# A hybrid encoder layer: the end of the first sweep, with one gate's products ahead of the last chunk's inner products and two pieces of element work behind `Ah`

## The chip, the cores and the metric

The kernel runs on one core of a Trainium2 chip. The core has five engines that each work through a list of instructions of their own, in order: TensorE (PE, with its weight loads shown apart as PEld), VectorE (DVE), ScalarE (ACT), GpSimd (POOL) and SyncE (SP), which here only issues DMAs. The metric is the device time of one execution in microseconds. Before the change it is 1314.11 us, the median of 3 runs from 1314.02 to 1314.79 us.

## The reference, cut to what matters

One layer projects `x` (2048 x 1024) into two groups of heads, mixes tokens in both, and joins them in one output projection and a LayerNorm.

```python
h = x @ w_in
(g_q, g_k, g_v, g_gate, g_lr_f, g_lr_b, m_cq, m_ckv, m_kr, m_gate) = split(h)
o_a = gla_branch(...)          # gated linear attention, forward and backward scans
o_b = mla_branch(...)          # latent attention with softmax
x = layer_norm(ALPHA * x + concat([o_a, o_b]) @ w_out)

# inside the linear attention, per chunk, b = cumsum(log_a):
q_dec, k_dec, k_tail = qc * exp(b), kc * exp(-b), kc * exp(b_last - b)
attn = where(mask, q_dec @ k_dec.T, 0.0)         # the inner products
o_intra = attn @ vc
state = state * exp(b_last) + k_tail.T @ vc
o = rms_norm(o_fwd + o_bwd) * silu(g_gate)
```

## The kernel before, in words

Every float32 product is made of three matmuls on a high and a low part of both operands (`mm3`, lines 420 to 422). ACT writes the high part (`hi`, line 366), and DVE or POOL the difference (`lo`, line 372). A pair therefore costs one ACT instruction and one DVE or POOL instruction, and the names end in `h` and `l`.

The work has three stages. **Sweep A** goes over 16 chunks of 128 positions from the last to the first (`c` from 15 to 0, step `i` from 0 to 15) and makes the projections of the linear attention (`ipa`), its decays, the inner products `Ap`, their masked form `At` with its parts `Ah` and `Al`, the products with the values (`Op`, then `oi`), the chunk's state `Up` and `Us`, and the gate: products `ipg` with the gate weights `wgh`, `wgl`, then the three ACT passes and one DVE pass of SiLU (tile `gs`). Results go to scratch in DRAM. Three gates are left for the end of the sweep: that of chunk 0 (`ipg` on `xah`, `xal`), which runs while the last chunk's own chain is finished, and those of chunks 15 and 14 (`late_gates`, on `xbh`, `xbl`, SiLU tile `ub`). **Sweep C** takes pairs of chunks forward: projections `ipm` and `pz`, the weights `pabs`, and per chunk the state products `Ob` that finish the linear attention. **Attention** and the output projection follow.

Three things set the order of the work around the change. In sweep A the order of writing mostly sets it, and `after(...)` holds what is written inside it behind a named instruction. In `late_gates` the splits of the weights `wm` and `wz`, of the first two input tiles (`xch`, `xcl`), and the SiLU of the two late gates are merged by two written lists, `TAIL_ACT` and `TAIL_DVE`. Sweep C starts behind these lists, ordered by the table `PLACE_C`.

At the end of sweep A, `run("intra", i)` (`ga_intra`, line 979) issues the twelve `Ap` matmuls, `At` on ACT (L987) and on DVE (L989), `Ah` on ACT and `Al` on DVE. Two buffers hold split inputs for the gates, so the split of chunk 14 (`xbh` on ACT, `xbl` on DVE, both 128x1024) goes into the buffer that chunk 0's gate still reads, and waits for that gate's last matmul. `load_x` keeps two raw input tiles, so the load of the second `xcf` waits on SP for `xbl`. POOL's multiplication of `Us` (L1030) follows DVE's `Us` (L1028).

Later names: `wml` and `wzl` are DVE's eight low parts of `wm` and of `wz`; `Sf` and `SU` on POOL (L1387, L1390, L1395) are sweep C's running state and the stored states that come back from DRAM; `MMb` and `qlb` are the operands of `Ob` (L1418, L1419).

Of the kernel before, what the change touches and what calls it, by code (L numbers as in the profile page):

```python
# [22 lines left out]
NCH = S // P  # L23
# [332 lines left out]
class K:  # L356
# [254 lines left out]
    def sweep_a(self):  # L611
        tc, nc, ins, cp = self.tc, self.nc, self.ins, self.cp
        with ExitStack() as ctx:
# [55 lines left out]
            g1 = ctx.enter_context(tc.tile_pool(name="g1", bufs=1))  # L669
# [3 lines left out]
            ch = self.ch = [dict(cst, c=NCH - 1 - i, i=i, lr=lrs[i % 2]) for i in range(NCH)]  # L673
            self.wa = wa
            run = lambda n, i: [0 for _ in getattr(self, "ga_" + n)(ch[i])]
# [24 lines left out]
            for t in ORDER_A.split():  # L700
                n, i = t.split(".")
# [21 lines left out]
            i = NCH - 1  # L723
# [3 lines left out]
            for k in self.gate_products(0, *ch[i]["x"], ip):  # L727
                if k == 5:
                    run("kt", i)
                    run("intra", i)  # L730
            self.gate_end(0, g1)
            run("state", i)
            run("av", i)

# [244 lines left out]
    def ga_intra(self, d):  # L979

        nc, c = self.nc, d["c"]
        Ap = d["gp"].tile([P, H, 2, P], F32, tag="gp", name=f"Ap{c}")
        for h in range(H):
            self.mm3(Ap[:, h], d["kh"][:, h], d["kl"][:, h], d["qbh"][:, h], d["qbl"][:, h])
        yield
        At = self.t512(d, "At")
        nc.scalar.activation(At, Ap[:, :, 1], AF.Copy)  # L987
        yield
        nc.vector.copy_predicated(At, d["mask"][:, None, :].to_broadcast([P, H, P]), Ap[:, :, 0])  # L989
        yield  # L990
        Ah = d["Ah"] = self.t512(d, "Ah", dt=F32R)
        self.hi(Ah, At)
        yield
        Al = d["Al"] = self.t512(d, "Al", dt=F32R)
        self.lo(Al, At, Ah)
        yield
# [62 lines left out]
    def late_gates(self):  # L1059

        tc, nc, ins, bc = self.tc, self.nc, self.ins, self.bc
        self.xch = bc.tile([P, NK, 2, P], F32R, name="xch")
        self.xcl = bc.tile([P, NK, 2, P], F32R, name="xcl")
        self.wqr_h = bc.tile([P, 2, 256], F32R, name="wqr_h")
        self.wqr_l = bc.tile([P, 2, 256], F32R, name="wqr_l")
        self.wabs_h = bc.tile([P, 2, H, P], F32R, name="wabs_h")
        self.wabs_l = bc.tile([P, 2, H, P], F32R, name="wabs_l")
        wm = self.load_ws(self.wm, [ins["wB"][k, :, 512:960] for k in range(NK)], 448, "wm")
        wz = self.load_ws(self.wz, [ins["wB"][k, :, 960:1472] for k in range(NK)], 512, "wz")
        next(wm)  # L1070
        with self.part("x14"):
            self.xlate.append(self.split_x(self.xab, self.xraw, NCH - 2, "xb", "dve"))
        next(wz)
        xc = self.load_x(0, "xc", 2)
        with self.part("wm"):
            self.Wm = next(wm)
        self.late_gate(NCH - 1, *self.xlate[0], self.ip)
        with self.part("c0"):
            self.split_c(xc[0], 0, "dve")
        with self.part("c1"):  # L1080
            self.split_c(xc[1], 1, "dve")
        self.late_gate(NCH - 2, *self.xlate[1], self.gp)
        with self.part("wz"):
            self.Wz = next(wz)
        self.tail = {e: self.merge(e, names) for e, names in zip(ENGINES[1:], (TAIL_ACT, TAIL_DVE))}
# [923 lines left out]
```

## Time and profile before

| | |
|---|---|
| median of the runs | 1314.11 us (1314.02 to 1314.79) |
| the profiled execution | 1313.98 us |
| its span | 1312.0 us |
| PE busy | 1288.9 us, 98% |
| DVE busy | 963.2 us, 73% |
| ACT busy | 812.9 us, 62% |
| POOL busy | 785.0 us, 60% |
| granted TensorE clock | 0.998 |
| sweep A's last steps and late gates | about 355 to 373 us of the span |

The busy shares are means over stages with different limits. In a row of the timeline the first number is the start in us from the span's begin, the second the duration in us; then come the engine, the line, the operation, the tiles written and read, the shapes, and in brackets the idle time before it with what ended that wait. Neighbouring rows of one kind are merged into one, with their count behind an x. Matmuls overlap one another, so their spacing is read from their starts.

### The profile page before, as it was taken

What the parts mean: (1) busy time and instruction counts of PE and PEld (TensorE: products, weight loads), DVE (VectorE), ACT (ScalarE), POOL (GpSimd) and SP (SyncE); (2) the same over time, 40 slices, a digit from 0 to 9 for tenths busy, and PEclk for the clock granted to TensorE, in tenths of its full rate; (3) what the DMA queues carried; (4) which work ended last, traced back from release to release, by engine and by line L of the source; (5) the groups of instructions that cost most, each with busy time, mean ns of one, the idle gap of its engine ahead of it and who ended that gap; (6) DMA issues with size and microseconds to landing.
All of it is one profiled execution on the core that took longest, in us unless ns stands there. A gap on an engine that the chain in (4) does not pass through costs nothing.

```text
span 1312.0 us, 19984 instructions
## 1 busy us (share of the span) xinstructions
PE 1288.9 (98%) x7081; PEld 1130.2 (86%) x7081; DVE 963.2 (73%) x1712; ACT 812.9 (62%) x1339; POOL 785.0 (60%) x494
## 2 busy tenths in 40 slices
PE   7999999999999999999999999999999999999997
PEld 7999999999889999999788888888888887788886
DVE  7967685655675455555888888888888888469997
ACT  6765656555575656664787877888888888511110
POOL 0143333232467666671388888889999999764441
PEclk9999999999999999999999999999999999999999
DMA  8132313132475555655401111122223110576662
GB/s 283 63 99 55 92 53 93 49 80 66 152 245 173 193 192 177 204 198 184 114 1 41 41 42 41 41 57 64 58 70 101 48 41 9 89 234 200 216 193 97
DMA packets 107819, 145.81 MB, mean 111 GB/s; under 512 B 17250, under 2 KB 62694, under 8 KB 107720
## 3 DMA queue, kind: packets, MB, share of 16 engines
q1 hardware_dynamic: 99128, 142.41, 35.3%
q0 software_dynamic: 672, 2.10, 0.4%
q8 instruction: 56, 0.92, 0.3%
q10 hardware_dynamic: 7920, 0.03, 0.3%
q14 instruction: 43, 0.35, 0.2%
HBM read 94.14 MB, written 50.36 MB: 110 GB/s over the span
## 4 chain that ended last, share of the span: by engine, by line
PE 65%; ACT 2%; POOL 1%; DMA 1%; DVE 1%; issue 0%; SPq 0%; DVEq 0%; ACTq 0%; POOLq 0%
PE pS L1521 4%; PE pS L1524 4%; PE pS L1523 4%; PE pS L1525 4%; PE o L420 4%; PE pS L1522 4%; PE o L422 4%; PE o L421 4%; PE po L421 2%; PE po L422 2%; PE po L420 2%; PE pz L421 2%; PE pz L420 2%; PE pz L422 2%; PE ipm L422 2%; PE ipm L420 2%
## 5 line engine op out<-in xcount | busy, mean ns | idle before, releaser
L372 POOL TENSOR_TENSOR pl<-s,ph 128x1024 fp32r<-128x1024 f32 x128 | 306.8, 2411 | 67.0 <-ACT ph L366 61.8
L1543 DVE TENSOR_TENSOR rm<-pS,rm 128x512 f32<-128x512 f32 x210 | 144.9, 690 | 44.2 <-ACT s L1530 39.0
L1530 ACT ACTIVATE s<-pS 128x1024 f32<-128x1024 f32 x128 | 131.4, 1026 | 67.9 <-PE pS L1525 65.9
L1567 DVE TENSOR_TENSOR s<-s,mb 128x1024 f32<-128x1024 f32 x128 | 151.2, 1213 | 9.5 <-PE mb L1561 9.3
L1030 POOL TENSOR_TENSOR Us<-Us,cw 128x512 f32<-128x512 f32 x16 | 18.5, 1157 | 226.7 <-DVE Us L1028 174.9
L366 ACT ACTIVATE ph<-s 128x1024 fp32r<-128x1024 f32 x128 | 135.0, 1056 | 16.7 <-PE o L422 16.1
L1571 ACT ACTIVATE s<-s 128x1024 f32<-128x1024 f32 x128 | 131.4, 1050 | 13.8 <-DVE s L1567 13.7
L420 PE MATMUL ipa<-wah,xah 128*128 128x384 f32 (+1 forms) x384 | 130.9, 341 | 6.1 <-ACT wah L366 5.9
L422 PE MATMUL ipa<-wah,xal 128*128 128x384 f32 (+1 forms) x384 | 125.3, 326 | 0.0
L421 PE MATMUL ipa<-wal,xah 128*128 128x384 f32 (+1 forms) x384 | 124.9, 325 | 0.0
L1521 PE MATMUL pS<-qh,ckvT_h 128*128 128x512 f32 x256 | 103.7, 405 | 0.7 <-ACT s L1571 0.4
L420 PE MATMUL o<-ph,vh 128*128 128x512 f32 x256 | 102.6, 401 | 0.0
L422 PE MATMUL o<-ph,vl 128*128 128x512 f32 x256 | 101.3, 396 | 0.0
L1524 PE MATMUL pS<-rh,krs 128*128 128x512 f32 x256 | 101.2, 395 | 0.0
L421 PE MATMUL o<-pl,vh 128*128 128x512 f32 x256 | 101.1, 395 | 0.0
L1523 PE MATMUL pS<-qh,ckvT_l 128*128 128x512 f32 x256 | 100.9, 394 | 0.0
L1525 PE MATMUL pS<-rl,krs 128*128 128x512 f32 x256 | 100.7, 393 | 0.0
L1522 PE MATMUL pS<-ql,ckvT_h 128*128 128x512 f32 x256 | 100.6, 393 | 0.0
L1594 DVE TENSOR_TENSOR ap<-ap,s 128x512 f32<-128x512 f32 x120 | 83.1, 692 | 7.0 <-ACT s L1571 5.1
L372 POOL TENSOR_TENSOR ol<-of,oh 128x512 fp32r<-128x512 f32 x32 | 43.1, 1347 | 61.5 <-ACT oh L366 61.5
L420 PEld LDWEIGHTS ipa<-wah,xah 128*128 128x128 f32 x384 | 73.6, 192 | 7.2 <-ACT wah L366 6.4
L420 PE MATMUL pz<-xch,wzh 128*128 128x256 f32 x256 | 74.8, 292 | 0.0
(325 smaller groups left out, 3862.0 us busy)
## 6 DMA issues: line engine op xcount, KB each, us to landing
xcf<-xT_dram SPq DMA_DIRECT2D x16, 512.0 KB, 5.1
xr<-x_dram SPq DMA_DIRECT2D x16, 512.0 KB, 5.8
out_dram<-rr SPq DMA_DIRECT2D x32, 256.0 KB, 2.0
xaf<-xT_dram SPq DMA_DIRECT2D x14, 512.0 KB, 4.1
oib<-oi_s SPq DMA_DIRECT2D x16, 256.0 KB, 5.3
qdb<-qd_s SPq DMA_DIRECT2D x16, 256.0 KB, 4.4
SU<-su_s SPq DMA_DIRECT2D x16, 256.0 KB, 4.5
ub<-u_s SPq DMA_DIRECT2D x16, 256.0 KB, 4.8
```

Of the source, the lines that this page charges most:

```text
L366: return nc.scalar.activation(dst, src, AF.Copy).ins
L372: return e.tensor_tensor(dst, src, hi.bitcast(F32), ALU.subtract).ins
L420: mm(out, ah, bh, start=start, stop=False)
L421: mm(out, ah, bl, start=False, stop=False)
L422: mm(out, al, bh, start=False, stop=stop)
L1521: mm(ps[:, e], kh, qh, start=True, stop=False)
L1522: mm(ps[:, e], kh, ql, start=False, stop=False)
L1523: mm(ps[:, e], kl, qh, start=False, stop=False)
L1524: mm(ps[:, e], kr, rh, start=False, stop=False)
L1525: mm(ps[:, e], kr, rl, start=False, stop=True)
L1543: V.tensor_tensor(d["rm"], src[:, e], d["rm"], ALU.max)
L1567: V.tensor_tensor(s, s, d["mb"][:, None, :].to_broadcast([P, 2, QB]), ALU.subtract)
```

## The change

The last chunk's inner products are written behind all of chunk 0's gate products instead of in front of the last quarter of them. The end of that gate, and the split of chunk 14's input, are held behind the `Ah` of the last chunk.

```diff
             for k in self.gate_products(0, *ch[i]["x"], ip):
                 if k == 5:
                     run("kt", i)
-                    run("intra", i)
-            self.gate_end(0, g1)
+            run("intra", i)
+            with self.after(ch[i]["Ahi"]):
+                self.gate_end(0, g1)
             run("state", i)
...
-        self.hi(Ah, At)
+        d["Ahi"] = self.hi(Ah, At)
...
-        with self.part("x14"):
+        with self.part("x14"), self.after(self.ch[NCH - 1]["Ahi"]):
             self.xlate.append(self.split_x(self.xab, self.xraw, NCH - 2, "xb", "dve"))
```

On PE, at the end of sweep A, the list was as follows (`kt` is the transposed keys, `Ap` the inner products, of which the first three of twelve stand here, `ipg` the gate, of whose six last matmuls the first three).

```order
L970 MATMUL kt_4053<-ident,kd_4015 128x128 x4
L420 MATMUL Ap_4062<-qbh_222,kh_4017 128x256
L421 MATMUL Ap_4062<-qbl_223,kh_4017 128x256
L422 MATMUL Ap_4062<-qbh_222,kl_4019 128x256
...
L420 MATMUL ipg_4034<-wgh_459,xah_3570 128x512
L421 MATMUL ipg_4034<-wgl_839,xah_3570 128x512
L422 MATMUL ipg_4034<-wgh_459,xal_3571 128x512
```

It is now this.

```order
L971 MATMUL kt_4053<-ident,kd_4015 128x128 x4
L420 MATMUL ipg_4034<-wgh_459,xah_3570 128x512
L421 MATMUL ipg_4034<-wgl_839,xah_3570 128x512
L422 MATMUL ipg_4034<-wgh_459,xal_3571 128x512
L420 MATMUL ipg_4034<-wgh_460,xah_3570 128x512
L421 MATMUL ipg_4034<-wgl_863,xah_3570 128x512
L422 MATMUL ipg_4034<-wgh_460,xal_3571 128x512
L420 MATMUL Ap_4068<-qbh_222,kh_4017 128x256
```

Six gate matmuls moved from behind the twelve `Ap` matmuls to the front of them. Behind both stands `Up` as before, then the gate of chunk 15; the first `Op` matmul, which needs `Ah`, stands behind four of that gate's matmuls instead of one.

On ACT at the same place the list was this (`gs` is chunk 0's gate, `xbh` the split of chunk 14).

```order
L987 ACTIVATE At_4075<-Ap_4062 128x512
L366 ACTIVATE xbh_4160<-xbf_3810 128x1024
L366 ACTIVATE Ah_4078<-At_4075 128x512
L1477 ACTIVATE gs_4088<-ipg_4034 128x512
L1026 ACTIVATE Us_4103<-Up_4094 128x512
L1479 ACTIVATE gs_4088<-gs_4088 128x512
L1481 ACTIVATE gs_4088<-gs_4088 128x512
L1008 ACTIVATE oi_4120<-Op_4111 128x512
L366 ACTIVATE wmh_4184<-wmr_4144 128x448
```

It is now this.

```order
L988 ACTIVATE At_4081<-Ap_4068 128x512
L366 ACTIVATE Ah_4084<-At_4081 128x512
L1478 ACTIVATE gs_4088<-ipg_4034 128x512
L1027 ACTIVATE Us_4103<-Up_4094 128x512
L1480 ACTIVATE gs_4088<-gs_4088 128x512
L366 ACTIVATE xbh_4160<-xbf_3810 128x1024
L1482 ACTIVATE gs_4088<-gs_4088 128x512
L1009 ACTIVATE oi_4120<-Op_4111 128x512
L366 ACTIVATE wmh_4184<-wmr_4144 128x448
```

The split of chunk 14 moved from in front of `Ah` to behind the second pass of the gate, four instructions later.

On DVE the list was this.

```order
L989 COPY_PREDICATED At_4075<-mask,Ap_4062 128x512
L372 TENSOR_TENSOR xbl_4161<-xbf_3810,xbh_4160 128x1024
L372 TENSOR_TENSOR Al_4080<-At_4075,Ah_4078 128x512
L1028 TENSOR_TENSOR Us_4103<-Up_4094,Us_4103 128x512
L1483 TENSOR_TENSOR gs_4088<-ipg_4034,gs_4088 128x512
L1010 TENSOR_TENSOR oi_4120<-Op_4111,oi_4120 128x512
L372 TENSOR_TENSOR wml_4192<-wmr_4144,wmh_4184 128x448
```

It is now this.

```order
L990 COPY_PREDICATED At_4081<-mask,Ap_4068 128x512
L372 TENSOR_TENSOR Al_4086<-At_4081,Ah_4084 128x512
L1029 TENSOR_TENSOR Us_4103<-Up_4094,Us_4103 128x512
L372 TENSOR_TENSOR xbl_4161<-xbf_3810,xbh_4160 128x1024
L1484 TENSOR_TENSOR gs_4088<-ipg_4034,gs_4088 128x512
L1011 TENSOR_TENSOR oi_4120<-Op_4111,oi_4120 128x512
L372 TENSOR_TENSOR wml_4192<-wmr_4144,wmh_4184 128x448
```

`xbl` moved from in front of `Al` and `Us` to behind them. The lists of POOL and SP, and all lists outside this place, are the same.

## The prediction, as it was recorded before the result was known

> **What bounds the kernel now.** The page comes first: PE is busy for 98% of the span at a granted clock of 1.00, so only waits of PE, and what stands behind them, can move the end. Then the chain of waits, read forward from the edited place, and the timeline of each engine there. The chain runs through other engines than PE shortly behind the late gates:
>
> ```profile
> 383.16 0.62 ACT MMb L366
> ...
> 385.14 1.25 POOL qlb L372
> 386.44 0.33 PE Ob L1419
> ```
>
> ```profile
> 386.44 0.33 PE L1419 MATMUL Ob<-MMb,qlb 128*128 128x128 f32 x1 [0.74 <-POOL qlb L372]
> ```
>
> The reader is to see that at 386.44 PE stands still for 0.74 us, for an operand from POOL that began as ACT's `MMb`. Time that PE wins before 386.44 makes this wait longer; what delays ACT or POOL ahead of it moves the end. From `Ob` on PE, ACT and POOL hand work to one another in fixed order, so I take a delay there as passed on whole.
>
> At the edited place PE does wait:
>
> ```profile
> 355.73 0.36 PE L420 MATMUL Ap<-qbh,kh 128*128 128x256 f32 x1
> ...
> 356.95 0.39 PE L422 MATMUL Ap<-qbh,kl 128*128 128x256 f32 x1 [0.34 <-DVE kl L372]
> ...
> 357.18 0.28 PE L420 MATMUL Ap<-qbh,kh 128*128 128x256 f32 x1
> ...
> 358.12 0.28 PE L422 MATMUL Ap<-qbh,kl 128*128 128x256 f32 x1
> ...
> 359.63 0.28 PE L1022 MATMUL Up<-VV,kth 128*128 128x256 f32 x1
> ...
> 360.50 0.44 PE L420 MATMUL ipg<-wgh,xbh 128*128 128x512 f32 x1
> ...
> 361.23 0.39 PE L1004 MATMUL Op<-VV,Ah 128*128 128x256 f32 x1 [0.29 <-ACT Ah L366]
> ...
> 362.62 0.29 PE L1005 MATMUL Op<-VV,Al 128*128 128x128 f32 x1
> ...
> 363.43 0.44 PE L420 MATMUL ipg<-wgh,xbh 128*128 128x512 f32 x1
> ```
>
> The first three `Ap` take 1.45 us, from 355.73 to 357.18, because their operands are late. The next nine start every 0.117 us.
>
> **The change, step by step.** *PE.* Six gate matmuls go in front; behind the last `Ap` start they and one `Ap` step fill 358.12 to 359.63, so they take 1.39 us. `Ap` then begins at 355.73 + 1.39 = 357.12, when `kl` has been there since 356.95, and needs 12 x 0.117 = 1.41: `Up` starts at 358.53 instead of 359.63. That is 1.10 us won. `Up` takes 0.87 (359.63 to 360.50) and four gate matmuls 0.93, so PE reaches `Op` at 360.33.
>
> *ACT.* Its rows in the timeline:
>
> ```profile
> 358.44 0.60 ACT L987 ACTIVATE At<-Ap 128x512 f32<-128x512 f32 x1 [1.84 <-PE Ap L422]
> 359.60 1.06 ACT L366 ACTIVATE xbh<-xbf 128x1024 fp32r<-128x1024 f32 x1 [0.56 <-PE ipg L421]
> 360.56 0.61 ACT L366 ACTIVATE Ah<-At 128x512 fp32r<-128x512 f32 x1
> ...
> 361.56 0.59 ACT L1026 ACTIVATE Us<-Up 128x512 f32<-128x512 f32 x1
> 362.04 0.63 ACT L1479 ACTIVATE gs<-gs 128x512 f32<-128x512 f32 x1
> 362.70 0.63 ACT L1481 ACTIVATE gs<-gs 128x512 f32<-128x512 f32 x1
> 363.63 0.60 ACT L1008 ACTIVATE oi<-Op 128x512 f32<-128x512 f32 x1 [0.29 <-PE Op L1005]
> 364.12 3.58 ACT L366 ACTIVATE wmh<-wmr 128x448 fp32r<-128x448 f32 x7
> 368.19 0.58 ACT L366 ACTIVATE wmh<-wmr 128x448 fp32r<-128x448 f32 x1 [0.49 <-DVE wml L372]
> ...
> 379.20 0.63 ACT L366 ACTIVATE wzh<-wzr 128x512 fp32r<-128x512 f32 x1 [1.66 <-DMA qdb<-qd_s]
> ```
>
> The last `Ap` moves from 358.12 to 358.41, so `At` to about 358.74. DVE's part of `At` follows 0.63 later and takes 0.74 (below), so `Ah` starts at about 360.15: 0.41 earlier than now. PE waits for it until about 360.8 and for `Al` until 361.5, and reaches the row of 363.43 at 362.35, a lead of 1.08. ACT goes on at the steps of the rows: `Us` 1.00 behind `Ah` at 361.15, the second `gs` at 361.63, `xbh` half a us on at 362.17 (before: 359.60), the third `gs` 0.96 behind it at 363.13, `oi` at 363.67, `wmh` at 364.16. ACT itself is as late as now: it loses no time and wins none, since the wait for the gate that it no longer has is replaced by a wait for `At`.
>
> *DVE* is different:
>
> ```profile
> 359.07 0.74 DVE L989 COPY_PREDICATED At<-mask,Ap 128x512 f32<-128x512 int32 x1 [0.97 <-ACT At L987]
> 360.69 1.23 DVE L372 TENSOR_TENSOR xbl<-xbf,xbh 128x1024 fp32r<-128x1024 f32 x1 [0.88 <-PE Up L1023]
> 361.84 0.69 DVE L372 TENSOR_TENSOR Al<-At,Ah 128x512 fp32r<-128x512 f32 x1
> 362.44 0.68 DVE L1028 TENSOR_TENSOR Us<-Up,Us 128x512 f32<-128x512 f32 x1
> ...
> 364.26 0.69 DVE L1010 TENSOR_TENSOR oi<-Op,oi 128x512 f32<-128x512 f32 x1 [0.20 <-ACT oi L1008]
> 364.86 4.57 DVE L372 TENSOR_TENSOR wml<-wmr,wmh 128x448 fp32r<-128x448 f32 x8
> ...
> 374.40 7.66 DVE L372 TENSOR_TENSOR wzl<-wzr,wzh 128x512 fp32r<-128x512 f32 x8
> ```
>
> ```profile
> 377.41 1.76 DVE L372 TENSOR_TENSOR wzl<-wzr,wzh 128x512 fp32r<-128x512 f32 x1
> ```
>
> ```profile
> 363.21 1.03 POOL L1030 TENSOR_TENSOR Us<-Us,cw 128x512 f32<-128x512 f32 x1 [4.87 <-DVE Us L1028]
> ...
> 377.06 1.55 POOL L1390 TENSOR_TENSOR Sf<-Sf,SU 64x512 f32<-64x512 f32 x1 [4.27 <-DMA SU<-su_s]
> 378.69 1.37 POOL L1395 TENSOR_TENSOR SU<-Sf,cw 64x512 f32<-64x512 f32 x1
> ```
>
> Now `xbl` lies in a hole of DVE. After the change it can begin when `xbh` ends, 362.17 + 1.06 = 363.23, behind which stand `gs`, `oi` and the eight `wml`. It also meets POOL's `Us`, which follows DVE's `Us` (361.78) by 0.77 and runs from 362.55 to 363.58. That such a meeting costs time is shown by the `wzl` rows: the first five start every 0.60 us, the sixth, which meets POOL, takes 1.76 instead of 0.68 and ends 0.56 behind POOL's end at 378.61, and three such end at 382.06, so each takes 0.92 more than 0.60. I take `xbl` as held to 363.58 and done at about 364.7; two more steps of 0.60 from 364.6 bring the first `wml` to 365.80: **0.94 us late**. If it isn't held, 0.75, since no row shows this very pair; I keep 0.94, as the `wzl` rows are nearest. [...] No gain is possible here, as ACT's `oi` is not earlier.
>
> The eighth `wmh` at 368.19 waits for DVE, so ACT takes the same 0.94 over, with `xch` and the rest of the written list behind it. The `wzl` start at 375.34 and the fourth at 377.14. The eighth `wzh` starts at 379.20, just when the sixth `wzl` ends (377.41 + 1.76 = 379.17); the row names a DMA, but DVE's end fits, and ACT's next rows lead without a hole to `MMb` at 383.16.
>
> How much is added to 0.94 hangs on POOL, whose four `Sf` and `SU` instructions begin when a load lands (377.06) and then alternate with the `wzl`. Before, the sixth, seventh and eighth `wzl` met them. With `wzl` 0.94 later and POOL not moved, one or two more of the first six meet them: POOL is asked for at 377.06 and the fourth `wzl` at 377.14. If POOL wins, the fourth, fifth and sixth meet it: 0.94 + 2 x 0.92 = 2.78 at the eighth `wzh`. If DVE wins, two do: 0.94 + 0.92 = 1.86. The rows can't part these by 0.1 us; I take the middle, **2.3 us**.
>
> *PE again.* It needs the eighth `wzl` at this row:
>
> ```profile
> 382.42 0.28 PE L422 MATMUL pz<-xch,wzl 128*128 128x256 f32 x1
> ```
>
> With its lead it gets there at 381.34, and the `wzl` ends at 382.06 + 0.94 + 0.92 = 383.92. The lead is gone and PE is 1.5 late, still less than `Ob` at 386.44 + 2.3. So PE's 1.08 is worth nothing.
>
> *Queues.* The load of the second `xcf` on SP waits for `xbl`, so it goes out 2.8 us later, with SP's list behind it:
>
> ```profile
> SPq L1141 <- DMA su_s<-Us: 3.1, 1, 3.1
> ...
> SPq L482 <- DVE xbl L372: 3.3, 1, 3.3
> ```
>
> ```profile
> xcf<-xT_dram SPq DMA_DIRECT2D x16, 512.0 KB, 5.1
> ```
>
> Out at 364.7 and landed 5.1 us later it is there at 369.8, before ACT's second `xch`, which comes behind the eighth `wmh` (369.1) and four more instructions of `TAIL_ACT`: no cost. Behind it SP stood 3.1 us for the store of `Us`, which covers the shift, and that store now goes out 0.66 earlier. So `SU` may land earlier by up to 0.7, or later by about as much because 0.5 MB of load comes behind instead of ahead. I take no shift.
>
> **The sum.** 1313.98 (this execution; the median is 0.13 higher) + 0.94 + 1.4 = **1316.3 us**, 0.17% above 1314.11. I call 0.2%, 2.6 us, what a measurement of this kernel tells from no change; so the forecast is a small loss just within it.
>
> **Rivals.**
> *`SU` lands late* (377.8 or later): POOL meets only the sixth to eighth `wzl`, as now, and 0.94 is all: 1314.9. For it: `xcf` lies ahead in the queue. Against: the store ahead of it is earlier.
> *`SU` lands early* (before 376.5): the third `wzl` is held too, 0.94 + 3 x 0.92 = 3.7: 1317.7.
> *The clock.* PE now waits in pieces of 1 to 2 us between 380.8 and `Ob`. The trace has a hole of 1.4 us near 1137 with full clock, and after PE's last matmul the clock falls:
>
> ```profile
> 1136.00:1140.00 4.00, 2.60 (x12) 1.82 (x11) 1.40 (x2) 3.32 (x4) 3.39 (x2) 1.00 0.01 1
> 1305.00:1312.00 7.00, 0.00 (x0) 0.00 (x0) 3.78 (x11) 0.41 (x2) 0.00 (x0) 0.63 0.19 75
> ```
>
> A mean of 0.63 over 7 us is 5.2 us at half rate. If the new waits did this, 5.2 us at half rate would lose 2.6 more: 1318.9. The longest single wait that I count is 1.8, so I give it little. [...]
> *Not slower.* PE's lead reaches the end: then 1313.98 - 1.08 = 1312.9. It needs the first `wml` at 364.86 or before, so `xbl` done by 363.7, one us earlier than its input allows by ACT's steps, and ACT's chain to `MMb` earlier as well. Only then does `Ob` not hold PE. Equal time, 1314.0, would be the first half of that.
>
> **How the numbers follow.** The pile-up with one or two more meetings (1315.8 to 1316.8) 0.48; `SU` late (1314.9) 0.18; `SU` early (1317.7) 0.16; clock 0.06; not slower 0.12. The range reaches from just under the late case to just over the early one, 1314.3 to 1318.3, and leaves out the clock and not slower, together 0.18. Slower by over 0.2%, above 1316.7: early, clock and 0.21 of the pile-up, 0.43. Faster by over 0.2%, below 1311.5: more than PE's lead, 0.05. Within: 0.52.
>
> **What would show it.** Right: `Ap` without a wait and `Up` near 358.5; `xbl` at or behind 363.2 and the first `wml` near 365.8; POOL `Sf` near 377 with four long `wzl`; the eighth `wzh` past 380.5; PE waiting at `pz` and about 2 us at `Ob`, near 388.7. Wrong: a first `wml` near 364.9, or `Ob` near 386.4 or before.

## The result, and the profile after

The changed kernel takes 1316.88 us (median of 21 runs, 1315.56 to 1318.09), the kernel before 1314.53 us (21 runs beside them, 1313.15 to 1316.80). The ratio is 1.0018, with a 95% interval from 1.0011 to 1.0024: a small loss of 1.4 to 3.2 us. The forecast was 1316.3 with a range of 1314.3 to 1318.3, a loss of 2.3.

The profiled executions differ by more, 1316.0 us of span against 1312.0. Part of that lies ahead of the edited place: the last `kt`, the last transposed keys before it, starts at 355.37 before and at 356.27 after. So all positions below are counted from the start of the last `kt` of the same trace. The table holds such positions, each the start of a row (in the last line its end) less the start of the `kt` row (us).

| | before | after | difference |
|---|---|---|---|
| PE `Up`, first | 4.26 | 3.24 | -1.02 |
| DVE `xbl` of chunk 14 | 5.32 | 7.95 | +2.63 |
| DVE first `wml` | 9.49 | 10.49 | +1.00 |
| DVE first `wzl` | 19.03 | 20.02 | +0.99 |
| POOL `Sf` of L1390, behind the load of `SU` | 21.70 | 21.73 | +0.03 |
| DVE sixth `wzl` | 22.04 | 24.94 | +2.90 |
| ACT eighth `wzh` | 23.83 | 26.50 | +2.67 |
| POOL `qlb` | 29.72 | 32.39 | +2.67 |
| PE second `Ob` matmul | 31.07 | 33.73 | +2.66 |
| POOL first `xcl` of sweep C | 43.83 | 46.47 | +2.64 |
| PE first scores `pS` of the attention | 260.67 | 263.55 | +2.88 |
| DVE end of the last `rr`, which the last store of the output follows | 953.62 | 956.76 | +3.14 |

So 2.66 us come from the edited place and are handed on. The other 1.4 us of the profiled difference are 0.90 ahead of it and 0.5 scattered far behind it. Whether any of the 0.90 belongs to the change stays open: second traces have this `kt` at 354.22 before and at 355.25 after, and in the other kernels that hold the change it lies anywhere from 354.85 to 356.21. The loss of the medians, 2.35, agrees with the 2.66 within its interval.

The timeline of the engines after the change, first DVE and POOL. (Lines behind the edit have a number one higher than before.)

```profile
356.27 0.60 PE L971 MATMUL kt<-ident,kd 128*128 128x128 f32 x4
```

```profile
364.22 1.43 DVE L372 TENSOR_TENSOR xbl<-xbf,xbh 128x1024 fp32r<-128x1024 f32 x1 [0.78 <-ACT xbh L366]
365.56 0.68 DVE L1484 TENSOR_TENSOR gs<-ipg,gs 128x512 f32<-128x512 f32 x1
366.17 0.67 DVE L1011 TENSOR_TENSOR oi<-Op,oi 128x512 f32<-128x512 f32 x1
366.76 4.55 DVE L372 TENSOR_TENSOR wml<-wmr,wmh 128x448 fp32r<-128x448 f32 x8
...
376.29 8.91 DVE L372 TENSOR_TENSOR wzl<-wzr,wzh 128x512 fp32r<-128x512 f32 x8
```

```profile
363.53 1.03 POOL L1031 TENSOR_TENSOR Us<-Us,cw 128x512 f32<-128x512 f32 x1 [4.27 <-DVE Us L1029]
...
378.00 1.29 POOL L1391 TENSOR_TENSOR Sf<-Sf,SU 64x512 f32<-64x512 f32 x1 [3.32 <-DMA SU<-su_s]
379.37 1.37 POOL L1396 TENSOR_TENSOR SU<-Sf,cw 64x512 f32<-64x512 f32 x1
380.81 1.37 POOL L1388 TENSOR_TENSOR Sf<-Sf,cw 64x512 f32<-64x512 f32 x1
382.26 1.60 POOL L1391 TENSOR_TENSOR Sf<-Sf,SU 64x512 f32<-64x512 f32 x1
```

Two things are to be seen. `xbl` waits for ACT's `xbh` and then overlaps POOL's `Us`; it takes 1.43 instead of 1.23, and with `gs` and `oi` behind it the first `wml` starts at 366.76. And the eight `wzl` take 8.91 us where they took 7.66.

ACT's three last `wzh` and the `MMb` that begins the chain to `Ob` (chain of waits), then that chain's end:

```profile
377.59 0.63 ACT L366 ACTIVATE wzh<-wzr 128x512 fp32r<-128x512 f32 x1 [0.62 <-DVE wzl L372]
379.87 0.63 ACT L366 ACTIVATE wzh<-wzr 128x512 fp32r<-128x512 f32 x1 [1.65 <-DVE wzl L372]
382.77 0.63 ACT L366 ACTIVATE wzh<-wzr 128x512 fp32r<-128x512 f32 x1 [2.26 <-DVE wzl L372]
```

```profile
386.71 0.62 ACT MMb L366
...
387.41 1.29 POOL MMb L372
388.70 1.26 POOL qlb L372
...
390.00 0.33 PE Ob L1420
```

Here the row names DVE's `wzl` as what the eighth `wzh` waits for, where the row of before had named a DMA. The chain to `Ob` is the one of before, later.

PE, and its granted clock in three stretches of the trace (columns: us, busy time and count of PE, PEld, DVE, ACT, POOL, granted clock, DMA share, GB/s):

```profile
382.79 0.39 PE L422 MATMUL pz<-xch,wzl 128*128 128x256 f32 x1 [0.82 <-DVE wzl L372]
...
384.47 0.58 PE L422 MATMUL pz<-xch,wzl 128*128 128x256 f32 x1 [1.06 <-DVE wzl L372]
...
390.00 0.33 PE L1420 MATMUL Ob<-MMb,qlb 128*128 128x128 f32 x1 [0.30 <-POOL qlb L372]
```

```profile
380.89:384.30 3.41, 1.69 (x11) 1.21 (x10) 3.41 (x3) 1.50 (x3) 2.90 (x2) 1.00 0.26 75
384.30:387.71 3.41, 3.24 (x14) 3.17 (x15) 2.48 (x7) 3.28 (x9) 0.63 (x2) 0.50 0.29 84
387.71:391.12 3.41, 3.11 (x26) 2.90 (x25) 1.67 (x8) 2.76 (x10) 3.41 (x4) 1.00 0.66 223
```

PE waits 0.82 and 1.06 us for the `wzl`, and at 384.30, in the second of these waits, the clock falls to half for 3.41 us. By an estimate from these rows (half of 3.41) that makes PE 1.7 us slower there, but at `Ob` it waits for `qlb` anyway: 0.30 us are left of that wait. The fall is hidden.

### The profile page after: what moved, and what is told of

It is laid out like the page before. It is cut to its first block, busy times and chain, and to the rows that moved or that the text cites. A ratio compares the mean times of both kernels' runs of the same rounds, so it can differ in the third digit from the quotient of the medians.

```text
span 1316.0 us, 19983 instructions
## 1 busy us (share of the span) xinstructions
PE 1290.3 (98%) x7081; PEld 1130.7 (86%) x7081; DVE 964.2 (73%) x1712; ACT 812.8 (62%) x1339; POOL 784.8 (60%) x494
## 4 chain that ended last, share of the span: by engine, by line
PE 84%; POOL 4%; ACT 3%; DVE 2%; issue 2%; DMA 1%; DVEq 0%; POOLq 0%; ACTq 0%
PE pS L1522 4%; PE pS L1525 4%; PE o L420 4%; PE o L422 4%; PE pS L1524 4%; PE o L421 4%; PE pS L1526 4%; PE pS L1523 4%; PE ipa L420 4%; PE ipa L422 4%; PE ipa L421 4%; PE pz L421 2%; PE pz L422 2%; PE pz L420 2%; PE po L421 2%; PE po L422 2%
```

## The experiments

Each kernel is the changed kernel with one more edit, unless it is said otherwise. A ratio is to the kernel before in runs on the same chip. The holds alone, `xbl` on POOL, no hold with SP in order, and the state loads later shared a chip with 33 runs of the kernel before (median 1315.70); the other four shared another with 26 (1316.09). The table gives the positions that decide, from the last `kt` of each trace.

| | first `wml` | `Sf` behind the load | all eight `wzl` take | eighth `wzh` | second `Ob` | first `xcl` | ratio, 95% interval |
|---|---|---|---|---|---|---|---|
| before | 9.49 | 21.70 | 7.66 | 23.83 | 31.07 | 43.83 | 1 |
| after | 10.49 | 21.73 | 8.91 | 26.50 | 33.73 | 46.47 | 1.0018 [1.0011, 1.0024] |
| holds alone | 9.51 | 23.64 | 5.08 | 22.77 | 31.67 | 44.43 | 0.9994 [0.9985, 1.0003] |
| `xbl` on POOL | 9.67 | 23.71 | 7.66 | 25.80 | 33.03 | 45.78 | 1.0014 [1.0005, 1.0023] |
| no hold on chunk 14, SP in order | 8.87 | 20.63 | 8.77 | 24.07 | 31.30 | 44.06 | 0.9990 [0.9981, 0.9999] |
| no hold on chunk 14, SP as it falls | 9.04 | 28.36 | 5.08 | 23.56 | 37.12 | 49.77 | 1.0030 [1.0018, 1.0042] |
| state loads later | 10.49 | 23.41 | 6.00 | 23.74 | 32.17 | 46.43 | 1.0016 [1.0007, 1.0026] |
| POOL's `qlb` early | 10.49 | 21.73 | 6.99 | 25.66 | 32.56 | 46.20 | 1.0022 [1.0012, 1.0032] |
| chunk 14 early, state later | 8.87 | 21.59 | 6.82 | 22.12 | 30.30 | 43.05 | 0.9987 [0.9978, 0.9997] |
| the same and `qlb` early | 8.87 | 21.36 | 5.98 | 22.12 | 29.24 | 42.70 | 0.9992 [0.9983, 1.0000] |

**The holds alone.** The products back in their old place, the two holds kept. What it tells apart: whether the moved products or the held split make `wml` late.

```diff
                 if k == 5:
                     run("kt", i)
-            run("intra", i)
+                    run("intra", i)
             with self.after(ch[i]["Ahi"]):
```

> The inner products go back in front of the last quarter of the gate; the two holds behind Ah stay. My theory (the loss is DVE's low part of the chunk-14 split, late by ACT's order and behind it the weights' low parts): here that split comes only one ACT instruction behind the gate's first pass, DVE has it at about 362 of the old time line, and the first wml stands 9.5 to 9.7 us behind the transposed keys kt, against 9.49 in the profile before and 10.49 after. Time as before, 1314.3 to 1315.3 us. Rival (the holds alone cost it, wherever the products stand): first wml at 10.4 or later, 1316.5 us or more.

With `Ap` early again, `xbl` starts at 6.57 and the first `wml` at 9.51, as before. So holding the split behind `Ah` costs `wml` nothing when the products stand in their old place (`Ah` starts at 4.48 here, at 4.84 in the changed kernel, and ACT takes the split two instructions earlier); it is the two together that push `xbl` behind `Us`. The `Sf` of POOL came 1.94 later than before, since the loads of `SU` went out 1.9 later on SP:

```profile
354.84 0.60 PE L971 MATMUL kt<-ident,kd 128*128 128x128 f32 x4
```

```profile
364.35 4.57 DVE L372 TENSOR_TENSOR wml<-wmr,wmh 128x448 fp32r<-128x448 f32 x8
...
373.89 5.08 DVE L372 TENSOR_TENSOR wzl<-wzr,wzh 128x512 fp32r<-128x512 f32 x8
```

```profile
378.49 1.63 POOL L1391 TENSOR_TENSOR Sf<-Sf,SU 64x512 f32<-64x512 f32 x1 [6.21 <-DMA SU<-su_s]
```

All eight `wzl` had started by then, and they take 5.08: this is what they take alone. Before, 7.66 minus 5.08 is 2.58 for three that meet POOL, 0.86 each; after, 8.91 minus 5.08 is 3.83 for four, 0.96 each. Yet `Ob` is 0.60 later than before, although ACT's eighth `wzh` is 1.06 earlier: now POOL, whose four instructions began late, is what `qlb` waits for. The ratio cannot be told from 1.

**`xbl` on POOL.** It takes the instruction off DVE without moving anything else on DVE.

```diff
         with self.part("x14"), self.after(self.ch[NCH - 1]["Ahi"]):
-            self.xlate.append(self.split_x(self.xab, self.xraw, NCH - 2, "xb", "dve"))
+            self.xlate.append(self.split_x(self.xab, self.xraw, NCH - 2, "xb"))
```

> The changed kernel with the low part of the chunk-14 split made by POOL in place of DVE; POOL is otherwise idle there. If DVE's own time is all that the split costs, wml begins 9.6 us behind kt (after: 10.49) and the time falls back to 1314.5 to 1315.5 us. If DVE and POOL exclude each other when both read SBUF, the first wml is held until POOL's 2.4 us are over, about 11.4 us behind kt, and three or four wzl meet POOL's running state as well: 1317.5 to 1319.5 us. My theory says the second.

```profile
365.41 2.42 POOL L372 TENSOR_TENSOR xbl<-xbf,xbh 128x1024 fp32r<-128x1024 f32 x1
```

```profile
365.29 0.68 DVE L1011 TENSOR_TENSOR oi<-Op,oi 128x512 f32<-128x512 f32 x1
365.89 2.43 DVE L372 TENSOR_TENSOR wml<-wmr,wmh 128x448 fp32r<-128x448 f32 x1
```

The first `wml` starts 0.82 earlier than in the changed kernel, but takes 2.43 us instead of 0.6. POOL's `xbl` ends at 367.83 (365.41 + 2.42), and `wml` 0.49 behind that: nearly the whole of it was waited out. The second `wml` starts at 12.03, 1.00 later than after and 2.00 later than before. So this `wml` did not run beside POOL's `xbl`, which had begun 0.48 before it; it stood until that was done. Three `wzl` met POOL, as expected, but the loss by the ratio is 0.7 to 3.0 us, where the expected times are 3.0 to 5.0 above the kernel before at 1314.5: the state landed 2.01 later than before as well, and `Ob` comes 0.70 earlier than in the changed kernel.

**Chunk 14 early, with SP's order kept.** The hold on the split is taken out, so `xbl` goes into the hole in front of `Al`; the second `xcf` load is tied behind the last `wz` load, so that it doesn't hold the other loads.

```diff
-        with self.part("x14"), self.after(self.ch[NCH - 1]["Ahi"]):
+        with self.part("x14"):
             self.xlate.append(self.split_x(self.xab, self.xraw, NCH - 2, "xb", "dve"))
         next(wz)
-        xc = self.load_x(0, "xc", 2)
+        last = self.nc.cur_bb.bb.instructions[-1]
+        xc = self.load_x(0, "xc")
+        with self.after(last):
+            xc += self.load_x(1, "xc")
```

> The changed kernel without the hold on the chunk-14 split (so that ACT and DVE split chunk 14 in the hole ahead of the last At), with the loads on SP kept in their old order. The products stay behind the gate and the gate's end behind Ah. My theory: the first wml comes 8.6 us behind kt (before 9.49, after 10.49), the first six wzl meet POOL's running state not at all, the eighth wzh comes about 2 us earlier than before, PE's lead of 1.1 us is used, and Ob comes 1.2 to 1.8 us earlier than before: 1312.7 to 1313.4 us. Rival (the products' new place is itself the loss): 1316 us or more.

The first `wml` comes 0.62 earlier than before, and so do the `wzl` up to the fifth. What was missed: the state landed 1.06 earlier too, and POOL met two of the first six `wzl` instead of one. The eighth `wzh` is 0.24 later than before:

```profile
373.55 8.77 DVE L372 TENSOR_TENSOR wzl<-wzr,wzh 128x512 fp32r<-128x512 f32 x8
```

```profile
375.78 1.41 POOL L1394 TENSOR_TENSOR Sf<-Sf,SU 64x512 f32<-64x512 f32 x1 [3.83 <-DMA SU<-su_s]
```

DVE is 0.62 early, and the eight `wzl` take 1.11 more than before. `Ob` moves by only +0.23. The start of the `wml` and the meetings with POOL are two separate terms, and the second swallowed the first. The runs have a ratio of 0.9990 all the same, close to the time that was expected, but not for the reason given: the positions it was to come from (`Ob` 1.2 to 1.8 earlier) were missed, so that agreement is luck. The traced execution is the slowest of its eleven, with a fall of the clock far behind (0.50 from 1140.91 to 1144.33); what the others gained, and where, stays open.

**Chunk 14 early, SP as it falls.** The same without the tie: the second `xcf` load stands ahead of others on SP and waits there for `xbl`.

```diff
-        with self.part("x14"), self.after(self.ch[NCH - 1]["Ahi"]):
+        with self.part("x14"):
```

> The changed kernel without the hold on the split of chunk 14, and with SP's list as it then comes: the second `xcf` load stands ahead of the `wm` loads and waits on SP for `xbl`, so these loads go out later. Theory (the late `xbl` alone makes the first `wml` late): first `wml` at 8.9 to 9.5 from the start of the last `kt` unless the `wm` loads are late; `Ob` between 29.9 and 31.5; 1314 to 1317 us, middle 1315. Rival (the queue order matters): the `wm` loads that stand behind the wait land after they are needed, ACT's `wmh` wait for DMA, and `Ob` is later than 32.

```profile
SPq L482 <- DVE xbl L372: 22.1, 1, 22.1
```

```profile
363.28 0.58 ACT L366 ACTIVATE wmh<-wmr 128x448 fp32r<-128x448 f32 x1 [0.32 <-DMA wmr<-wB_dram]
```

```profile
381.44 0.55 PE L1166 MATMUL pabs<-wkr,wqT 128*128 128x128 f32 x1 [4.84 <-DMA wqT<-wqT_dram]
```

The rival was right. SP stands 22.1 us for `xbl`, and the loads of the weights and of the state stand behind it. ACT's `wmh` wait for DMA in five pieces, PE waits 4.84 us for `wqT`, and `Ob` is 6.05 later than before. An edit of one hold moved a load on SP ahead of the rest of its list, and that cost `Ob` more than the whole change does. The ratio shows less of it, 2.4 to 5.5 us; where the rest was won back is not shown.

**State loads later.** In the changed kernel the loads of `SU` and the POOL work on them are placed later in sweep C's table (`lS`, `M`, `Sf1`, `Sf2`).

```diff
-    M=(-0.426, 0.04),
-    Sf1=(-1.303, -0.348),
-    Sf2=(-0.613, -0.339),
+    M=(-0.18, 0.04),
+    Sf1=(-1.303, -0.175),
+    Sf2=(-0.19, -0.17),
...
-    lS=(-1.12, -1.093),
+    lS=(-0.2, -0.195),
```

> The changed kernel with the two loads of the stored states put behind the store of the first late gate on SP, so that POOL's running state begins 3 us or more later and meets few of the first six wzl. My theory: with the meetings gone the eighth wzh comes 24 us behind kt in place of 26.5 (before: 23.83), that is 0.2 to 0.6 later than before instead of 2.7; POOL is then the last to be ready, Ob comes about 32.3 us behind kt (before 31.07, after 33.73), 1315.0 to 1316.3 us. Rival (the meetings cost nothing, the 2.7 us come from the split alone): eighth wzh at 26 or more, Ob at 33.7 or more, 1316.9 us or more.

The first `wml` stays at 10.49, and none of the first six `wzl` meets POOL. The eighth `wzh` comes at 23.74 instead of 26.50. That is 0.09 earlier than in the kernel before, whose `wml` start 1.00 earlier but whose sixth `wzl` meets POOL. So 1.00 of the loss at the eighth `wzh` is `wml`, and the rest the meetings. `Ob` gains 1.56 and comes at 32.17, because POOL now bounds it:

```profile
386.45 0.39 PE L1419 MATMUL Ob<-MMb,qhb 128*128 128x256 f32 x1 [1.61 <-POOL MMb L372]
...
387.68 0.33 PE L1420 MATMUL Ob<-MMb,qlb 128*128 128x128 f32 x1 [0.84 <-POOL qlb L372]
```

In this trace the clock then stood at 0.51 from 389.21 to 392.63, behind `Ob`, where PE had no wait to spare, and by the first `xcl` the gain was gone (46.43 against 46.47). The positions decide for the theory; the time does not decide. The ratio is a loss of 0.9 to 3.4 us, which fits the theory's times (0.5 to 1.8 above 1314.5) as well as the rival's (2.4 or more), and whether the clock fell like this in all ten runs is not shown.

**POOL's `qlb` early.** In the changed kernel, the order of POOL's list alone is altered: `qlb`, `MMb` and `krf` ahead of the second pair of `Sf`.

```diff
-    Sf1=(-1.303, -0.348),
-    Sf2=(-0.613, -0.339),
-    qlb=(-0.023, 0.63),
+    Sf1=(-1.303, -0.1),
+    Sf2=(-0.613, -0.09),
+    qlb=(-0.115, 0.63),
...
-    krfa=(-0.119, 0.94),
+    krfa=(-0.108, 0.94),
```

> The changed kernel with the order of POOL's list alone altered: behind `SU` of L1395 stand `qlb`, `MMb`'s low part and `krf`, and only then the next `Sf` of L1387 and of L1390, so two of the four POOL instructions that alternate with the `wzl` move behind `qlb`. Times are counted from the start of the last `kt`. Theory (each `wzl` that meets a POOL instruction costs 0.92 more, and POOL's list ahead of `qlb` holds `Ob`): the `wzl` that meet POOL fall from five or so to two or three, the eighth `wzh` comes at about 25.6 instead of 26.50, `qlb` loses its wait for POOL, and the second `Ob` starts at about 32.3 instead of 33.73; about 1.4 us less than the changed kernel, a ratio to the kernel before of about 1.0007. Rival (the meetings cost nothing at the end, the late first `wml` and the chain behind it alone set `Ob`): `Ob` stays within 0.3 of 33.7.

The eighth `wzh` comes at 25.66 (expected 25.6), 0.84 earlier: one meeting less among the first six. `Ob` comes at 32.56, of the 1.4 expected 1.17. But the first `xcl` is only 0.27 earlier than after. POOL does behind `qlb` what it did ahead of it:

```profile
385.74 1.27 POOL L372 TENSOR_TENSOR qlb<-qdb,qhb 128x512 fp32r<-128x512 f32 x1 [5.31 <-ACT qhb L366]
386.97 1.26 POOL L372 TENSOR_TENSOR MMb<-SU,MMb 128x512 fp32r<-128x512 f32 x1
388.19 0.32 POOL L1296 TENSOR_TENSOR krf<-krf,rope 128x64 f32<-128x64 f32 x1
388.47 1.03 POOL L1388 TENSOR_TENSOR Sf<-Sf,cw 64x512 f32<-64x512 f32 x1
389.58 1.28 POOL L1391 TENSOR_TENSOR Sf<-Sf,SU 64x512 f32<-64x512 f32 x1
```

From 385.74 on POOL's rows follow one another without a hole until past 401, and its `xcl` stands behind them. What `Ob` won was given back on POOL, and the runs show no gain: 1.0022.

**Chunk 14 early, state later.** The split early with SP's order kept, and the loads of `SU` behind the load of `oib`, about one microsecond later than in the kernel that had only the first part. Its edit is that kernel's, and:

```diff
-    Sf2=(-0.613, -0.339),
+    Sf2=(-0.448, -0.339),
...
-    lS=(-1.12, -1.093),
+    lS=(-0.45, -0.449),
```

> The changed kernel without the hold on the split of chunk 14 (first `wml` early, as in the run with that one hold taken out, with SP's order kept), and with the loads of the stored state behind the load of `oib` on SP, so that they land later. Times are counted from the start of the last `kt`; the kernel before has the first `wml` at 9.49, the eighth `wzh` at 23.83 and the second `Ob` at 31.07. Theory (the first `wml` and the number of `wzl` that meet POOL are two separate terms): first `wml` at 8.9; the state lands at 21.2 to 21.7 instead of 20.6, one meeting fewer; eighth `wzh` at 23.2, or 22.1 if two fewer; `Ob` at 29.7 to 30.5, 0.6 to 1.35 us before the kernel before. Rival (POOL's own list ahead of `qlb` is the bound as soon as the state lands later): `Ob` at 31.0 or later, no gain.

All as the theory had it: `wml` at 8.87, `Sf` at 21.59, the eighth `wzh` at 22.12, `Ob` at 30.30, 0.77 earlier than before. Its median is 1314.42 us against 1316.09 of the kernel before, a ratio of 0.9987 with an interval that ends below 1 (0.9978 to 0.9997). So it is faster than the kernel before, by 0.4 to 2.9 us, and by its ratio than the changed one too, whose ratio is from other runs. It has the lowest ratio of those run here, but the interval of the one with the split early alone overlaps with its own, so the runs do not show that the later load is worth time. What bounds `Ob` in it is POOL, as its chain of waits shows; in this the rival was right, but not in the time at which it bounds:

```profile
371.23 6.05 DMA SU<-su_s
377.43 1.65 POOL Sf L1394
379.15 1.37 POOL SU L1399
380.60 1.37 POOL Sf L1391
...
383.61 1.24 POOL MMb L372
384.85 1.24 POOL qlb L372
```

**The same, with `qlb` early.** On top of the last kernel, POOL's order as in the one ahead of it.

```diff
-    Sf1=(-1.303, -0.348),
-    Sf2=(-0.448, -0.339),
-    qlb=(-0.023, 0.63),
+    Sf1=(-1.303, -0.1),
+    Sf2=(-0.448, -0.09),
+    qlb=(-0.115, 0.63),
...
-    krfa=(-0.119, 0.94),
+    krfa=(-0.108, 0.94),
```

> The run above (split of chunk 14 early, state landing later) with POOL's `qlb`, `MMb` low part and `krf` ahead of the second `Sf` pair as well. Theory: POOL can no longer hold `qlb`, ACT's `MMb` does; `Ob` at about 29.85 from the start of the last `kt`, 1.2 us before the kernel before, ratio about 0.999. Rival: the `Sf` pair that now stands behind `qlb` delays the second pair's state products, and what `Ob` wins is given back there, ratio 1.000 or above.

`Ob` comes at 29.24, 1.82 earlier than before (1.2 expected). The first `xcl` is 1.13 earlier, so 0.7 is given back on POOL, as in the other kernel with this order. Then the clock fell at the output projection in both traces taken of this kernel (0.50 from 1139.11 to 1142.53 here; the second is below), and the ratio is 0.9992 with an interval that reaches 1. Against the kernel without this order it is not a gain that these runs show.

**Second traces.** The changed kernel, the kernel before and the last one were traced once more, for the clock, with nothing altered.

> The changed kernel once more, for a second trace of its clock. Theory (PE's waits at `pz` bring the fall of the granted clock behind the late gates): the same 3.4 us at half rate about 28 us behind the last `kt`. Rival (falls come with an execution, not with the change): full clock there. Either way the second `Ob` is at 33.7 from the last `kt`, since POOL's `qlb` and not PE sets it; with full clock PE waits there for about 1.8 us instead of 0.30.

> The kernel before once more, for a second trace. Theory: full clock around `Ob`, the second `Ob` at 31.1 from the last `kt`. The hole of PE at the start of the output projection, 1.4 us long, kept full clock in the first trace; if the falls there come with an execution, it may fall this time, and then the span is 2 to 2.5 us longer.

> The kernel with the split of chunk 14 early, the state landing later and `qlb` early on POOL, once more. Theory (the fall of the clock at the output projection comes with an execution): `Ob` at 29.2 again, the first `xcl` at 42.7, and if the clock stays full at the output projection, `pmb` at 787.0 instead of 789.1 from the last `kt`. Rival (the fall belongs to this kernel): `pmb` at 789.1 again.

The positions repeat: `Ob` at 33.73, 31.12 and 29.21. One repeats less well: in the two traces of the last kernel `Sf` behind the load starts at 21.36 and 22.18 and ends at 23.83 in both, so single starts of that row are rough. In the changed kernel the clock fell near the same place again, at 29.4 from `kt` where the first trace has 28.0, and `Ob` did not move. In the kernel before it fell in the second trace at the start of the output projection, where the first trace had full clock: `pmb`, a tile of that projection just behind, comes at 790.40 instead of 787.68, 2.2 of it between `po` and `pmb`. So in this kernel the fall comes with the execution. In the last kernel it fell there both times (0.51 from 1138.71 to 1142.13 in the second trace; `pmb` at 789.12 and 788.88), which alone does not part the two theories.

## Why the prediction was right, and where it was off

- **PE's lead** came as predicted: `Ap` without a wait, `Up` 1.02 earlier (1.10). In the changed kernel it is worth nothing, as predicted: PE loses more than the lead behind the `wzl` and still waits at `Ob`. The eight kernels with the same lead (`Up` at 3.24) have `Ob` anywhere between 29.24 and 37.12, so the lead alone does not set it.
- **`xbl` behind `Us`** was the right cause. Predicted were `xbl` at 7.86 from `kt` and the first `wml` at 10.43 (0.94 late); measured 7.95 and 10.49 (1.00 late). The holding by POOL's `Us` is seen: `xbl` starts 0.34 before POOL's `Us` ends and takes 1.43, where it takes 1.23 alone.
- **The meetings.** Left open was whether POOL or DVE wins at the fourth `wzl`. POOL won: the fourth, fifth and sixth are held, as in the case worked out to 2.78 at the eighth `wzh`; measured 2.67. The middle of 2.3 was taken for want of 0.1 us, and the true case is its upper one. That the medians differ by 2.35, so close to this middle, is therefore luck; their interval holds both cases, 1.86 and 2.78, and it is the positions that tell them apart. The price of a meeting, put at 0.92, came out at 1.08 for the fourth `wzl` and 0.85 for the fifth; the sixth, held in both kernels, takes 0.24 less than before. With the 0.98 by which the fourth `wzl` is late, 0.98 + 1.08 + 0.85 - 0.24 is the 2.67.
- **The state's load.** No shift was taken, and it moved by 0.03, although the load that waits for `xbl` went out 2.8 later; SP stood 5.7 us for `xbl` instead of 3.3 and no longer for the store of `Us`. The reading was not as safe as that makes it look: in four of the five other kernels that left the table's entry for this load alone, POOL's `Sf` behind it moved by -1.06, +1.94, +2.01 and +6.66, so the rivals *`SU` early* and *`SU` late* were real ones. Two runs made them happen: with the load 1.06 earlier a meeting more, with it 1.7 later none among the first six.
- **From `Ob` to the end** a delay was taken as passed on whole: 2.66 at `Ob`, 2.64 at `xcl`, 2.88 at the first scores. Two traces of the kernel before differ by 0.54 at that last place, so nothing finer can be read there. In time the step is less certain than in the traces: two kernels that win 1.56 and 1.17 at `Ob` against the changed one show no gain that their ratios can tell (1.0016 and 1.0022).
- **The clock** was the rival that happened, in its mechanism and not in its price. It was given little since no single wait was above 1.8 us, and it fell with waits of 0.82 and 1.06. The prediction priced it at 2.6 more; it cost an estimated 1.7 on PE (half of 3.41) and nothing at `Ob`, which waited for `qlb` in any case. So what was predicted as a wait of about 2 us at `Ob` shows as 0.30 and a slow stretch. That the length of the longest wait decides is not shown by any run; at the output projection a hole of 1.94 us was followed by a fall and one of 2.01 was not (last section).
- **Not slower** needed a first `wml` at 9.49 or before. The runs with the split early show that such a kernel is to be had: with the state landing as before, `Ob` is 0.77 earlier than before. The prediction's reason against it here, that ACT hands over `xbh` too late, held.

## What to carry to other kernels

Where instructions of two engines hold each other up, as DVE's `wzl` and POOL's `Sf` and `SU` did here at 0.86 to 0.96 us a meeting, a delay of one engine is not passed on as it is (0.98 at the fourth `wzl` became 2.67 at the eighth `wzh`): it changes how many of their instructions meet, so write down the times of both lists and count the meetings before and after. The landing of the load that starts the other engine's work is as strong a lever on the positions as the delay itself (2.76 us at the eighth `wzh`); that it is worth time is not shown here, since alone it won none that the runs can tell, and with the split early 0.9987 stands beside 0.9990 without it. And a hold on one instruction moves the DMAs that wait for it, with all that stands behind them in SP's list (SP stood 22.1 us for `xbl` in the run with SP as it falls): look there first.

## What the runs showed of the hardware

**In these traces the granted clock falls for stretches of 3.41 us, and the length of one wait does not part the falls from the rest.** In the changed kernel the clock is 0.50 from 384.30 to 387.71, and its fall at the kernel's end begins at 1312.72, 928.4 us behind the first: 272 times 3.413. In the run with SP as it falls two falls begin at 380.71 and 1145.31, 764.6 us or 224 times 3.413 apart. In nine of the thirteen traces ten falls ahead of the kernel's end were read, each at 0.50 or 0.51 over its first 3.42 us. In a fall the `pz` matmuls start 0.21 us apart and at full clock 0.12, the `po` matmuls 0.43 and 0.23, so PE's rows show where it ends; six end with the 3.42 us, and the first one with SP as it falls lasts to about 387.5, twice as long. Below, a stretch of 3.41 us that ends where a fall begins, or lies whole multiples of 3.413 from one, is called a window. How the windows lie differs from execution to execution: the fall of the changed kernel begins 28.0 us behind `kt` in one trace and 29.4 in the other.

The hole of PE at the start of the output projection shows what goes with a fall, here in the kernel before, first trace and second trace, and in the changed kernel's second trace. Each pair of rows is a window and the one behind it.

```profile
1136.19:1139.60 3.41, 2.01 (x9) 1.34 (x8) 1.40 (x2) 3.13 (x4) 2.99 (x2) 1.00 0.00 0
1139.60:1143.02 3.42, 3.42 (x16) 2.82 (x15) 0.00 (x0) 0.47 (x1) 3.42 (x3) 1.00 0.66 230
```

```profile
1135.93:1139.34 3.41, 1.47 (x6) 0.87 (x6) 1.40 (x2) 3.38 (x4) 2.74 (x2) 0.99 0.00 0
1139.34:1142.76 3.42, 3.42 (x9) 2.65 (x8) 0.00 (x0) 0.16 (x1) 3.42 (x3) 0.51 0.69 230
```

```profile
1138.98:1142.39 3.41, 1.55 (x7) 0.91 (x5) 1.40 (x2) 3.41 (x4) 2.28 (x1) 1.00 0.00 0
1142.39:1145.81 3.42, 3.28 (x14) 2.73 (x15) 0.00 (x0) 0.43 (x1) 3.42 (x3) 1.00 0.61 198
```

PE was busy for 2.01 us of the first window and the next kept full clock; for 1.47 us of the second, and the next ran at 0.51. Nineteen windows at full clock (1.00 or 0.99), away from the kernel's start and end, were read with the one behind them. Of the six in which PE was busy for 2.01 us or more (up to 2.66) none was followed by a fall. Of the nine with 1.58 us or less, eight were, and the third fence is the one that was not. Of the four between (1.68, 1.69, 1.76 and 1.92) two were, those with 1.69 and 1.92. PE's ends are modelled, so the bound is rough, about half of the window. The hole itself was 1.35 to 2.01 us long over the thirteen traces: behind 1.94 (second trace of the kernel before) the clock fell, behind 2.01 (second trace of the changed kernel) it did not. Nor was a window ahead of a fall idle, but for one with SP as it falls (0.00): in the other nine PE was busy for 1.42 to 1.92 of its 3.41 us.

The scatter of the runs goes with the clock too. Of the 26 runs of the kernel before on one chip, the ten with a mean clock of 0.999 have a median of 1314.83 us, the eleven with 0.997 one of 1316.66.

**In these rows a meeting costs DVE about what is left of POOL's instruction.** In the `wzl` rows after, the fourth starts when POOL's `Sf` has 1.20 us left, the fifth and sixth when `SU` and `Sf` have 0.97 left; they are held for 1.08, 0.85 and 0.85, and each ends 0.55 behind POOL's end. In the `xbl` run a `wml` starts when 1.94 of POOL's 2.42 are left, is held for 1.83 (2.43 against 0.6) and ends 0.49 behind it. POOL takes longer as well: its `Sf` with the state takes 1.28 behind the `wzl` (389.58 in the kernel with `qlb` early) and 1.60 beside them (382.26 in the changed kernel), and the profile shows this as the duration of the instruction and not as a wait.
